# A fixed order for TensorE in the RWKV-7 recurrence of a decoder trunk: small products behind each chain step, then four dense k-tiles

## The chip, the cores and the metric

The kernel runs on one core of a Trainium2 chip. The metric is the device time of one execution in microseconds (us). A run of the same program is repeated, and the median is taken. The kernel before the change takes 2544.87 us (median of three runs, 2544.0 to 2546.05).

## What is computed

A two-layer decoder trunk over 256 tokens with 2048 channels, in float32: an RWKV-7 time mixing layer, then a causal differential attention layer, each followed by a gated MLP with a short convolution, with layer norms between. The change lies wholly in the time mixing, whose core is this:

```python
def wkv7_scan(r, decay, k, v, a_vec, b_vec):
    def step(S, inp):
        r_t, w_t, k_t, v_t, a_t, b_t = inp
        sa = jnp.einsum('bhij,bhj->bhi', S, a_t)
        S = S * w_t[:, :, None, :] + sa[..., None] * b_t[:, :, None, :] + v_t[..., None] * k_t[:, :, None, :]
        y = jnp.einsum('bhij,bhj->bhi', S, r_t)
        return S, y
...
def rwkv7_mix(x, ...):
    r = xr @ w_rkv[0]; k = xk @ w_rkv[1]; v = xv @ w_rkv[2]
    w = -softplus(-(w0 + tanh(xw @ w1) @ w2)) - 0.5
    a = sigmoid(a0 + (xa @ a1) @ a2); g = sigmoid(xg @ g1) @ g2
    ...
    y = wkv7_scan(r_h, decay, k_h, v_h, -kk, kk * a_h)
    ...
    return (y * g) @ w_o
```

The r, k and v weights are 2048 by 2048; the scan runs over 32 heads of 64 channels, with `kk` normalised per head before it and a group norm per head and a bonus term behind it.

## The kernel before

**Dense products.** A 2048-wide product is cut into k-tiles of 128 rows. Each weight tile comes from memory as float32 (`raw`, by SyncE's queue), ScalarE (ACT) rounds it to TensorE's shorter float (fp32r) (`hi`, line 213), VectorE (DVE) forms the rest (`lo`, line 216), and TensorE (PE) multiplies. One `hi` and one `lo` tile hold two k-tiles; each of the three pools has six buffers in this part, so `lo` can run at most twelve k-tiles ahead. A k-tile costs PE either three matmuls of 256 columns (lines 224 to 226: twice with `hi`, once with `lo`; the r and k products of the recurrence) or one of 512 and one of 256 (lines 228 and 229; the output product w_o). The third of the first kind, line 226, is the one that needs `lo`.

**The recurrence.** The 2048 channels are handled in eight groups of 256 (four heads). A group passes four stages, written as Python generators that `yield` between steps:

- `products(g)` (line 1075): the r and k products of the group, 64 dense k-tiles, 20 steps.
- `front(g)` (line 1085): the elementwise work of the group, mostly on DVE with 512-wide tiles: norm of k (product of line 1107), decay factors, the scaled operands `KB` (lines 1139, 1140) and `AR` (1141, 1143); then 32 products of line 1152 that fill the chunk matrices `M` (DVE, line 1155). It also runs two of the three small low-rank products of a group (`lora`, line 822: lines 224 to 226 with the operand `mid`).
- `lanes(g)` (line 1188): the inverse of the triangular chunk matrices: four transposes (line 1211, twice), tiny DVE steps (1215, 1217), a trip through memory (1220, 1224), and six rounds of 16 or 32 tiny products (lines 1238, 1247, 1259, 1266, 1277, 1286), each round waiting for a copy or a transpose of the one before on ACT or DVE (the first for 1231, the second for the masking of line 1239).
- `chain(g)` (line 1308) and `outputs(g)` (line 1391): the four chunks of 64 tokens one after the other. Per chunk the products of lines 1353/1357 (with the state `S`) or 1342, a copy to `R`, line 1365, a copy to `UV`, line 1376 and a new `S` on DVE (1380, 1383), with 1386 adding to the result. Thirteen steps, each waiting for a copy of the one before. Then the group norm: line 1407 on PE, and on DVE and ACT 1409, 322 to 326, 1413, 1414. For the last three groups line 1414 is followed by the split of the result into `S1`, the operand of w_o (lines 194 and 195).

`pipeline` (line 1009) runs in round i the chain of group i, the lanes of i+1, the front of i+2 and the products of i+3 together. `_together` takes the next step of whichever generator has the smallest share done, by the step counts in `PACE`. In the last three rounds `early(n)` (line 1024) takes the place of the products: parts of the first fourteen columns of w_o whose inputs are already there.

**What sets the order.** The framework reorders at compile time: from the written program, its priorities and its own cost table it fixes one order of instructions per engine, and each engine executes its list in that order. All waits are semaphores put in by the framework. The low-rank products share one buffer each for the raw and the split weights (`lb=1`): the split of one (lines 828 on ACT, 830 on DVE) writes the buffer which the matmuls of the one before read. Small products of `front` and `lanes` write to a ring of two PSUM banks (`pst`).

The lines that call the scheduler's helper and set the pace, the rest being printed below:

```python
PACE = dict(chain=37.24, front=19.56, lanes=19.55, products=40.92, pool=0, pool0=0, chain0=0, front0=0,
...
    def pst(self):
        return self.pss.tile([P, 2 * T], F32, name="pss")
```

Of the kernel before, what the change touches and what calls it, by code (L numbers as in the profile page):

```python
# [14 lines left out]
P = 128  # L15
# [13 lines left out]
NC = T // C  # L29
GT = 2  # L30
NG = KT // GT
WCH = 4
HCH = 2
PACE = dict(chain=37.24, front=19.56, lanes=19.55, products=40.92, pool=0, pool0=0, chain0=0, front0=0,
            lanes0=0, early0=0, products0=0, wc='AVVA', ek='AA', ez='VA', ec='AVAA', ey='V', el='V', w0=(3, 4,
            4), lb=1, early=46.23, vw=(6, 6, 6), vp=2, ep='V', eg='A', lg=2, lr=2, la=4, ah=10, ao=12, ah0=0.05)
EARLY = {j: 0 if j < 5 else 1 if j < 11 else 2 for j in range(14)}
AGAIN = (2,)
ORDER = [0, 1, 14, 2, 3, 4, 5, 6, 7, 15, 8, 9, 10, 11, 12, 13]
# [89 lines left out]
class Trunk:  # L129
    def __init__(self, ctx, tc, a):  # L130
# [5 lines left out]
        self.wp = []  # L136
        self.weight_pools(ctx, "0", PACE["w0"])
        self.tmp = mk("tmp", 3)
# [478 lines left out]
    def attention(self, lead=None, ahead=None):  # L617
        nc, tc = self.nc, self.tc
        with ExitStack() as ctx:
# [18 lines left out]
            def query_steps(h, n=0):  # L638
                evac = queries(h)
                yield from self.dense_steps(self.qk_blocks(h)[n:], KT, self.S0, lambda j, ps: evac(j + n, ps))  # L640

            def values(h):
                def evac(ps):
                    vt = ap.tile([P, 2, 2, P], F32, name="vt")
                    nc.scalar.copy(out=vt, in_=ps.rearrange("p (a b c) -> p a b c", a=2, b=2))
                    qkv[h].append(vt)

                yield from self.token_steps(self.a["da_v"][h], self.S0, evac)
# [89 lines left out]
    def rwkv(self, ahead=None):  # L738
        nc, tc = self.nc, self.tc
        with ExitStack() as ctx:  # L740
# [192 lines left out]
def _all(steps):  # L933
    for _ in steps:
        pass


def _then(*steps):
    for s in steps:
        yield from s  # L940


def _together(*todo):

    at = [[o[0] if o else 0.0, i, s, 1.0 / n] for i, (s, n, *o) in enumerate(todo)]
    while at:
        m = min(at)
        try:
            next(m[2])
            m[0] += m[3]  # L950
        except StopIteration:
            at.remove(m)
# [10 lines left out]
class Groups:  # L963
# [44 lines left out]

    def pipeline(self):
        for i in range(-3, NG):  # L1010
            todo = []
            if i >= 0:
                todo.append((_then(self.chain(i), self.outputs(i)), PACE["chain"], PACE["chain0"]))
            if 0 <= i + 1 < NG:
                todo.append((self.lanes(i + 1), PACE["lanes"], PACE["lanes0"]))
            if 0 <= i + 2 < NG:
                todo.append((self.front(i + 2), PACE["front"], PACE["front0"]))
            if 1 <= i + 3 < NG:
                todo.append((self.products(i + 3), PACE["products"], PACE["products0"]))
            if i + 3 >= NG:  # L1020
                todo.append((self.early(i - (NG - 3)), PACE["early"], PACE["early0"]))
            _together(*todo)

    def early(self, n):

# [162 lines left out]
    def lanes(self, g):  # L1188

        t, nc, g1 = self.t, self.nc, self.g1  # L1190
        s = self.st[g]
        M, d1, d2, KB, pc = s["M"], s["d1"], self.d2, s["KB"], s["pc"]
        KBT = s["KBT"] = self.g2.tile([P, GT * NC, P], F32, name="KBT")
# [11 lines left out]
                                in1=pc.rearrange("p j c o -> p (j c) o").broadcast_to([P, GT * NC, 2 * C]),  # L1205
                                op=ALU.mult)
        yield
        for u in range(0, GT * NC, 4):
            ps = self.pst()
            for w in range(4):  # L1210
                nc.tensor.transpose(out=ps[:, w * P:(w + 1) * P], in_=KB[:, u + w, :, :], identity=t.c("ident"))
            self.copy(PACE["ek"][u // 4], KBT[:, u:u + 4, :].rearrange("p u c -> p (u c)"), ps)
            yield
        for i in range(1, 8):
            nc.vector.tensor_tensor(out=tt[:, :i, :i], in0=Tl[:, :i, :i],
                                    in1=Ml[:, 0:i, i].unsqueeze(1).broadcast_to([P, i, i]), op=ALU.mult)
# [4 lines left out]
        for par in range(2):  # L1221
            for be in range(2):
                r0 = (64 if par == 0 else 0) + 32 * be
                nc.sync.dma_start(out=W1[r0:r0 + 32],
                                  in_=self.dram(d2, par * 8, ((C, 32), (4 * DBL, 8), (1, 32)), at=be * 2 * DBL))
# [7 lines left out]
        ps = self.pst()  # L1233
# [9 lines left out]
        ps = self.pst()  # L1243
# [10 lines left out]
        ps = self.pst()  # L1254
# [7 lines left out]
        ps = self.pst()  # L1262
# [10 lines left out]
        ps = self.pst()  # L1273
# [8 lines left out]
        ps = self.pst()  # L1282
# [207 lines left out]
```

## Time and profile before

| what | value |
|---|---|
| median of three runs | 2544.87 us |
| the profiled execution's own time | 2540.27 us |
| its span from first to last instruction | 2537.5 us |
| mean granted TensorE clock | 0.99 |
| busy: PE / DVE / ACT | 2461.7 / 2030.6 / 1648.8 us |
| first product of line 1407 (output of group 0) | 277.51 us after the start of the span |
| last product of line 1407 (group 7) | 593.45 us |

Times in views are microseconds from the start of the span. PE means matmuls, PEld its weight loads. A matmul's own duration overlaps the next one's: in a stream the distance between starts counts, not the duration. An engine's "idle before" names what ended the idle time. In the table of stretches each engine has its busy time and the number of its instructions, then the granted clock and the load of the DMA engines. The eight products of line 1407 mark the rounds of the pipeline.

### The profile page before, as it was taken

What the parts mean: (1) busy time and instruction counts of PE and PEld (TensorE: products, weight loads), DVE (VectorE), ACT (ScalarE), POOL (GpSimd) and SP (SyncE); (2) the same over time, 40 slices, a digit from 0 to 9 for tenths busy, and PEclk for the clock granted to TensorE, in tenths of its full rate; (3) what the DMA queues carried; (4) which work ended last, traced back from release to release, by engine and by line L of the source; (5) the groups of instructions that cost most, each with busy time, mean ns of one, the idle gap of its engine ahead of it and who ended that gap; (6) DMA issues with size and microseconds to landing.
All of it is one profiled execution on the core that took longest, in us unless ns stands there. A gap on an engine that the chain in (4) does not pass through costs nothing.

```text
span 2537.5 us, 56569 instructions
## 1 busy us (share of the span) xinstructions
PE 2461.7 (97%) x18622; PEld 2170.2 (86%) x18622; DVE 2030.6 (80%) x5192; ACT 1648.8 (65%) x4334; POOL 172.0 (7%) x236
## 2 busy tenths in 40 slices
PE   7999999999899999999999999999999999999996
PEld 6988888777888888888889899988988888888886
DVE  8988888878997777776776977779887777776776
ACT  5766566545676666665666666666766666666664
POOL 1000000000300000000111200003300000000111
PEclk9999999999999999999999999999999999999998
DMA  6644343344465556666766455556465555566664
GB/s 189 187 141 120 110 108 102 106 127 125 133 198 189 190 190 190 190 190 196 215 188 188 149 167 174 171 176 184 147 198 188 188 188 188 188 187 186 188 190 128
DMA packets 276743, 428.70 MB, mean 169 GB/s; under 512 B 60632, under 2 KB 83168, under 8 KB 276448
## 3 DMA queue, kind: packets, MB, share of 16 engines
q1 hardware_dynamic: 276448, 425.10, 55.6%
q8 instruction: 145, 2.38, 0.4%
q14 instruction: 150, 1.23, 0.2%
HBM read 420.25 MB, written 6.31 MB: 168 GB/s over the span
## 4 chain that ended last, share of the span: by engine, by line
PE 81%; DVE 3%; ACT 1%; DMA 1%; issue 1%; SPq 0%; POOL 0%; ACTq 0%; DVEq 0%; POOLq 0%
PE psd L228 43%; PE psd L229 22%; PE psd L224 2%; PE psd L225 2%; PE psd L226 2%; PE psd L296 1%; PE psd L295 1%; PE psd L294 1%; PE psd L900 1%; PE psd L899 1%; PE psd L901 1%; DVE lo L216 1%; DMA raw<-in_rw_o 1%; PE lnst L348 1%; PE pss L1152 0%
## 5 line engine op out<-in xcount | busy, mean ns | idle before, releaser
L213 ACT CAST hi<-raw 128x256 fp32r<-128x256 f32 (+1 forms) x3128 | 1231.4, 404 | 682.1 <-PE psd L228 466.2
L216 DVE TENSOR_TENSOR lo<-raw,hi 128x256 fp32r<-128x256 f32 (+1 forms) x3124 | 1308.3, 430 | 418.9 <-ACT hi L213 375.9
L228 PE MATMUL psd<-S,hi 128*128 128x512 f32 x3004 | 1056.7, 396 | 0.8 <-DVE S L195 0.8
L229 PE MATMUL psd<-S,lo 128*128 128x256 f32 x3004 | 842.1, 280 | 3.9 <-DVE lo L216 3.8
L228 PEld LDWEIGHTS psd<-S,hi 128*128 128x128 f32 x3004 | 566.2, 189 | 132.8 <-ACT hi L213 1.3
L229 PEld LDWEIGHTS psd<-S,lo 128*128 128x128 f32 x3004 | 566.0, 188 | 5.6 <-DVE lo L216 5.3
L228 PE MATMUL psd<-hs,hi 128*128 128x512 f32 x1290 | 451.2, 394 | 0.0
L229 PE MATMUL psd<-hs,lo 128*128 128x256 f32 x1290 | 361.5, 280 | 0.0
L228 PEld LDWEIGHTS psd<-hs,hi 128*128 128x128 f32 x1290 | 241.8, 187 | 56.3 <-ACT hi L213 0.9
L229 PEld LDWEIGHTS psd<-hs,lo 128*128 128x128 f32 x1290 | 243.1, 188 | 0.4 <-DVE lo L216 0.3
L226 PE MATMUL psd<-S,lo 128*128 128x256 f32 x480 | 139.1, 290 | 2.9 <-DVE lo L216 2.8
L224 PE MATMUL psd<-S,hi 128*128 128x256 f32 x480 | 138.5, 289 | 1.6 <-ACT hi L213 1.4
L225 PE MATMUL psd<-S,hi 128*128 128x256 f32 x480 | 137.6, 287 | 0.0
L228 PE MATMUL psd<-S1r,hi 128*128 128x512 f32 x276 | 107.2, 419 | 2.0 <-ACT hi L213 1.0
L226 PEld LDWEIGHTS psd<-S,lo 128*128 128x128 f32 x480 | 90.7, 189 | 8.6 <-DVE lo L216 5.0
L224 PEld LDWEIGHTS psd<-S,hi 128*128 128x128 f32 x480 | 90.7, 189 | 6.4 <-ACT hi L213 2.3
L225 PEld LDWEIGHTS psd<-S,hi 128*128 128x128 f32 x480 | 90.6, 189 | 1.7 <-issue 1.4
L366 POOL COPY ln_acc<-X 128x256 f32<-128x256 f32 x4 | 2.0, 512 | 1239.3 <-DVE X L400 1239.3
L224 PE MATMUL psd<-S1r,hi 128*128 128x256 f32 x284 | 85.6, 301 | 0.0
L900 PE MATMUL psd<-S,lo 128*128 128x258 f32 x256 | 77.7, 303 | 8.1 <-DVE lo L216 8.1
L228 PE MATMUL psd<-S1a,hi 128*128 128x512 f32 x240 | 84.9, 398 | 0.0
L229 PE MATMUL psd<-S1r,lo 128*128 128x256 f32 x276 | 80.8, 293 | 1.5 <-DVE lo L216 1.5
(303 smaller groups left out, 3577.3 us busy)
## 6 DMA issues: line engine op xcount, KB each, us to landing
raw<-in_ff_up SPq DMA_DIRECT2D x676, 256.0 KB, 3.4
raw<-in_ff_down SPq DMA_DIRECT2D x320, 256.0 KB, 3.0
raw<-in_rkv SPq DMA_DIRECT2D x192, 256.0 KB, 3.6
raw<-in_da_qk SPq DMA_DIRECT2D x122, 256.0 KB, 3.4
raw<-in_da_v SPq DMA_DIRECT2D x64, 256.0 KB, 3.0
raw<-in_da_o SPq DMA_DIRECT2D x64, 256.0 KB, 3.7
raw<-in_rw_o SPq DMA_DIRECT2D x50, 256.0 KB, 3.3
raw<-in_ff_down SPq DMA_DIRECT2D x32, 192.0 KB, 2.6
```

What stands on the lines that cost most here:

```text
L213: nc.scalar.copy(out=hi[:, :s * P], in_=r)
L216: eng.tensor_tensor(out=lo[:, :s * P], in0=r, in1=hi[:, :s * P].bitcast(F32), op=ALU.subtract)
L224: nc.tensor.matmul(ps[:, :T], lhsT=hi, rhs=xs[:, :T], start=first, stop=False)
L225: nc.tensor.matmul(ps[:, :T], lhsT=hi, rhs=xs[:, T:], start=False, stop=False)
L226: nc.tensor.matmul(ps[:, :T], lhsT=lo, rhs=xs[:, :T], start=False, stop=last)
L228: nc.tensor.matmul(ps, lhsT=hi, rhs=xs, start=first, stop=False)
L229: nc.tensor.matmul(ps[:, T:], lhsT=lo, rhs=xs[:, :T], start=False, stop=last)
L294: nc.tensor.matmul(o, lhsT=xh, rhs=hi, start=k == 0 and b == 0, stop=False)
L295: nc.tensor.matmul(o, lhsT=xh, rhs=lo, start=False, stop=False)
L296: nc.tensor.matmul(o, lhsT=xl, rhs=hi, start=False, stop=k == KT - 1 and b == T // P - 1)
L348: self.nc.tensor.matmul(st, lhsT=self.c("onesd"), rhs=t, start=not self.ln_open and n == 0, stop=stop and n == 1)
L900: nc.tensor.matmul(ps[:, 2:4 + T], lhsT=lo[:, w], rhs=x[:, 2:4 + T], start=False, stop=False)
```

## The change

In rounds 0 to 7 TensorE keeps the order in which the source creates its instructions (`manual_schedule`); the other engines are still ordered by the framework. The source's order is rewritten: `abreast` takes one step of the chain (or of the outputs behind it), then steps of the lanes at a rate of 12/17 and of the front at 16/17 per chain step; `_together` sets this against the products with 18 and 20 steps, so that four dense k-tiles follow each chain step. `early` gets one step count for each of its three rounds. In `lanes` the two banks of transposes are issued together, and the copies behind them. Code below the change moves down: line numbers of `lanes`, `front` and `chain` grow by 16 to 18.

```diff
-PACE = dict(chain=37.24, front=19.56, lanes=19.55, products=40.92, pool=0, pool0=0, chain0=0, front0=0,
+PACE = dict(chain=18, front=19.56, lanes=19.55, products=20, pool=0, pool0=0, chain0=0, front0=0,
...
     def pipeline(self):
         for i in range(-3, NG):
-            todo = []
-            if i >= 0:
-                todo.append((_then(self.chain(i), self.outputs(i)), PACE["chain"], PACE["chain0"]))
+            todo, side = [], []
             if 0 <= i + 1 < NG:
-                todo.append((self.lanes(i + 1), PACE["lanes"], PACE["lanes0"]))
+                side.append((self.lanes(i + 1), PACE["lanes"], PACE["lanes0"]))
             if 0 <= i + 2 < NG:
-                todo.append((self.front(i + 2), PACE["front"], PACE["front0"]))
+                side.append((self.front(i + 2), PACE["front"], PACE["front0"]))
             if 1 <= i + 3 < NG:
                 todo.append((self.products(i + 3), PACE["products"], PACE["products0"]))
             if i + 3 >= NG:
-                todo.append((self.early(i - (NG - 3)), PACE["early"], PACE["early0"]))
-            _together(*todo)
+                n = i - (NG - 3)
+                todo.append((self.early(n), PACE["early"][n], PACE["early0"]))
+            if i < 0:
+                _together(*side, *todo)
+            else:
+                with self.t.tc.manual_schedule(engines={mybir.EngineType.PE}):
+                    _together((self.abreast(_then(self.chain(i), self.outputs(i)), [s for s, *_ in side]), PACE["chain"],
+                               PACE["chain0"]), *todo)
+
+    def abreast(self, main, side):
+
+        rates = dict(zip(side, (12 / 17, 16 / 17)) if len(side) > 1 else ((s, 12 / 17) for s in side))
+        due = dict.fromkeys(side, 0.0)
+        for _ in main:
+            for s in side:
+                due[s] += rates[s]
+                while due[s] >= 1:
+                    next(s, None)
+                    due[s] -= 1
+            yield
+        _all(_then(*side))
...
-        for u in range(0, GT * NC, 4):
-            ps = self.pst()
-            for w in range(4):
-                nc.tensor.transpose(out=ps[:, w * P:(w + 1) * P], in_=KB[:, u + w, :, :], identity=t.c("ident"))
-            self.copy(PACE["ek"][u // 4], KBT[:, u:u + 4, :].rearrange("p u c -> p (u c)"), ps)
-            yield
+        banks = [self.pst(), self.pst()]
+        for u in range(GT * NC):
+            nc.tensor.transpose(out=banks[u // 4][:, u % 4 * P:(u % 4 + 1) * P], in_=KB[:, u, :, :],
+                                identity=t.c("ident"))
+        for u, ps in enumerate(banks):
+            self.copy(PACE["ek"][u], KBT[:, 4 * u:4 * u + 4, :].rearrange("p u c -> p (u c)"), ps)
+        yield
```

**Place 1: DVE in the middle of the front of one group (steady rounds).** Before, DVE's list between the second copy to `R` and the fill of the scaled operands reads so; `lo_` with a number is one `lo` tile, `AR`, `wa`, `k`, `KB` are tiles of the front, `UV` and `R` belong to the chain.

```order
L1059 COPY R_2553<-b1_5502 128x64
L1127 SCALAR_TENSOR_TENSOR kk_5449<-k_4620,par_74,kk_5449 128x256
L1129 TENSOR_SCALAR t1_5448<-wa_5342,par_74 128x256
L1141 SCALAR_TENSOR_TENSOR AR_5444<-kk_5449,Lx_5532 128x8x64
L1132 TENSOR_TENSOR wa_5342<-kk_5449,wa_5342 128x512
L1133 SCALAR_TENSOR_TENSOR k_4620<-t1_5448,k_4620 128x512
L1059 COPY UV_2552<-us_5426 64x128
L216 TENSOR_TENSOR lo_5688<-raw_5685,hi_5687 128x256
L216 TENSOR_TENSOR lo_5698<-raw_5685,hi_5697 128x256
L216 TENSOR_TENSOR lo_5720<-raw_5717,hi_5719 128x256
```

The same place in the changed kernel, from the last `lo` tile ahead of these operations to the first behind them:

```order
L216 TENSOR_TENSOR lo_5642<-raw_5629,hi_5641 128x256
L1149 TENSOR_TENSOR wa_5167<-kk_5511,wa_5167 128x512
L1150 SCALAR_TENSOR_TENSOR k_4605<-t1_5510,k_4605 128x512
L1157 TENSOR_TENSOR KB_5667<-wa_5167 128x2x2x64
L1076 COPY UV_2552<-us_5434 64x128
L1156 TENSOR_TENSOR KB_5667<-k_4605,wa_5167 128x2x2x64 x2
L1157 TENSOR_TENSOR KB_5667<-wa_5167 128x2x2x64
L1158 SCALAR_TENSOR_TENSOR AR_5506<-kk_5511,Lx_5562 128x8x64
L1160 TENSOR_TENSOR AR_5506<-r_4999,eL_5563 128x8x64
L216 TENSOR_TENSOR lo_5677<-raw_5674,hi_5676 128x256
```

The three `lo` tiles which stood ahead of the four `KB` operations and the second `AR` operation now stand behind them. What PE has in its list between the last matmul with `lo_5642` and the first with `lo_5677` is this:

```order
L226 MATMUL psd_5444<-S0_76,lo_5642 128x256
L1383 MATMUL us_5434<-R_2553,M_3833 64x64 x4
L1360 MATMUL b0_5489<-UV_2552,M_3833 64x64 x2
L1360 MATMUL b1_5490<-UV_2552,M_3833 64x64 x2
L224 MATMUL psd_5444<-S0_76,hi_5676 128x256
L225 MATMUL psd_5444<-S0_76,hi_5676 128x256
L226 MATMUL psd_5444<-S0_76,lo_5677 128x256
```

Here one step of the chain (lines 1365 and 1342 of the kernel before) and two dense matmuls are all that stands between the two.

**Place 2: PE at the second and third low-rank product of a round.** Before, the second product (`mid0`, weights `l2_6179`) and the third (`mid1`, `l2_6236`) have other small products between them:

```order
L226 MATMUL psd_6183<-mid0_81,l2_6179 128x256
L1318 MATMUL us_6261<-ext_2531,X_75 128x128 x2
L1323 MATMUL us_6261<-ext_2531,X_75 64x128
L1277 MATMUL pss_6193<-T1_6190,M_4612 32x32 x16
L224 MATMUL psd_6240<-mid1_82,l2_6236 128x256
```

In the changed kernel they follow each other:

```order
L224 MATMUL psd_6086<-mid2_83,l2_6082 128x256
L225 MATMUL psd_6086<-mid2_83,l2_6082 128x256
L226 MATMUL psd_6086<-mid2_83,l2_6082 128x256
L224 MATMUL psd_6098<-mid1_82,l2_6094 128x256
L225 MATMUL psd_6098<-mid1_82,l2_6094 128x256
```

`l2_6082` and `l2_6094` are the same buffer, so the second's weights can be split only when the first's six matmuls are through.

**Place 3: PE behind the last product of line 1407.** Before, dense k-tiles of w_o follow whose inputs are there (`psd_9660`, and after it `psd_9688` and others, 44 k-tiles in all):

```order
L1407 MATMUL us_9747<-o_y2_9674,ext_2531 128x512
L228 MATMUL psd_9660<-S1r_80,hi_9663 128x512
L229 MATMUL psd_9660<-S1r_80,lo_9664 128x256
L228 MATMUL psd_9660<-S1r_80,hi_9663 128x512
L229 MATMUL psd_9660<-S1r_80,lo_9664 128x256
```

Now the k-tiles of the last group's own result follow at once (`psd_9975` and `psd_9989`, the first two columns of w_o):

```order
L1425 MATMUL us_9922<-o_y2_9835,ext_2531 128x512
L224 MATMUL psd_9975<-S1r_80,hi_9978 128x256
L224 MATMUL psd_9989<-S1r_80,hi_9992 128x256
L225 MATMUL psd_9975<-S1r_80,hi_9978 128x256
L226 MATMUL psd_9975<-S1r_80,lo_9979 128x256
```

The 44 k-tiles have moved ahead of line 1425, between the steps of the last chain.

More of the change, by code (lines that the diff above doesn't have):

```diff
@@ L33 @@
 HCH = 2
-PACE = dict(chain=37.24, front=19.56, lanes=19.55, products=40.92, pool=0, pool0=0, chain0=0, front0=0,
+PACE = dict(chain=18, front=19.56, lanes=19.55, products=20, pool=0, pool0=0, chain0=0, front0=0,
             lanes0=0, early0=0, products0=0, wc='AVVA', ek='AA', ez='VA', ec='AVAA', ey='V', el='V', w0=(3, 4,
-            4), lb=1, early=46.23, vw=(6, 6, 6), vp=2, ep='V', eg='A', lg=2, lr=2, la=4, ah=10, ao=12, ah0=0.05)
+            4), lb=1, early=(16, 25, 34), vw=(6, 6, 6), vp=2, ep='V', eg='A', lg=2, lr=2, la=4, ah=10, ao=12, ah0=0.05)
 EARLY = {j: 0 if j < 5 else 1 if j < 11 else 2 for j in range(14)}
```

## The prediction

> **What bounds the kernel now.** I read the page first:
>
> ```profile
> PE 2461.7 (97%) x18622; PEld 2170.2 (86%) x18622; DVE 2030.6 (80%) x5192; ACT 1648.8 (65%) x4334; POOL 172.0 (7%) x236
> ```
>
> PE is busy for 97%, so time goes where PE's list gets shorter, or where it waits. Outside the recurrence the order is unchanged, so I cut that part at the first products of line 1407 (before's numbers), one round per row; the last row runs from the eighth to PE's first product behind the recurrence.
>
> ```profile
> 277.51:325.67 48.16, 46.88 (x758) 40.20 (x757) 41.32 (x109) 30.67 (x74) 0.69 (x3) 1.00 0.41 108
> 422.19:470.66 48.47, 46.60 (x759) 40.06 (x757) 42.48 (x111) 32.95 (x78) 0.69 (x3) 1.00 0.40 107
> 470.66:514.59 43.93, 40.64 (x470) 30.69 (x469) 37.95 (x105) 26.15 (x64) 0.46 (x3) 1.00 0.37 106
> 514.59:563.99 49.40, 48.69 (x848) 37.17 (x847) 35.01 (x99) 23.56 (x60) 0.00 (x0) 0.90 0.46 123
> 593.45:617.55 24.10, 20.30 (x111) 16.19 (x109) 19.75 (x52) 11.87 (x31) 0.10 (x1) 1.00 0.54 158
> ```
>
> The first two rows are the first and last of four steady rounds: 193.15 us from 277.51 to 470.66, 48.3 each. PE is idle there for 1.3 and 1.9 us, and DVE is busy for 41 to 42 of the 48: a second engine with little room. PE's waits in the four rounds:
>
> ```profile
> PE pss L1286 <- ACT T L1279: 3.1, 4, 0.9
> PE pss L1107 <- DVE bon L1175: 1.1, 4, 0.3
> PE pss L1247 <- DVE M L1155: 0.6, 2, 0.3
> PE b L1353 <- DVE S L1383: 0.4, 1, 0.4
> ```
>
> These sum to 5.2, or 1.3 per round: all that waiting costs in the order of before.
>
> The rest of PE's time is its work, and in its timeline one sees what cutting the dense stream costs:
>
> ```profile
> 397.94 0.45 PE L1376 MATMUL us<-UV,KBT 128*64 128x64 f32 x8
> 398.22 0.40 PE L1386 MATMUL yps<-M,UV 128*64 128x64 f32 x8
> 398.55 0.38 PE L224 MATMUL psd<-S,hi 128*128 128x256 f32 x1
> 398.78 0.28 PE L225 MATMUL psd<-S,hi 128*128 128x256 f32 x1
> 398.90 0.28 PE L226 MATMUL psd<-S,lo 128*128 128x256 f32 x1
> ...
> 399.97 0.28 PE L226 MATMUL psd<-S,lo 128*128 128x256 f32 x1
> 400.18 0.34 PE L1353 MATMUL b<-S,AR 64*64 64x64 f32 x8
> ```
>
> Dense matmuls start 0.12 apart (398.78 to 398.90), but the first is followed after 0.23 and the last after 0.21. So a piece costs 0.09 to 0.11 at each end, 0.2 in all, beside its matmuls. This piece, four k-tiles, takes 1.63 (398.55 to 400.18).
>
> **The change part by part.** *Removed.* The 64 k-tiles of a round stood in some 20 pieces and stand in 15: five pieces by 0.2 is 1.0 less. The new order puts four k-tiles ahead of most products that waited, so the 1.3 of waits may go too. At most 2.4 per round (0 at the worst). I take 2.4.
>
> *Added: DVE's block in the front (Place 1).* DVE executes its list in order. Here are its operations as they ran before:
>
> ```profile
> 395.17 0.68 DVE L1141 SCALAR_TENSOR_TENSOR AR<-kk,Lx 128x512 f32<-128x512 f32 x1
> 395.77 0.68 DVE L1132 TENSOR_TENSOR wa<-kk,wa 128x512 f32<-128x512 f32 x1
> 396.38 0.68 DVE L1133 SCALAR_TENSOR_TENSOR k<-t,k 128x512 f32<-128x512 f32 x1
> 397.09 0.29 DVE L1059 COPY UV<-us 64x128 f32<-64x128 f32 x1
> 397.42 1.10 DVE L216 TENSOR_TENSOR lo<-raw,hi 128x256 fp32r<-128x256 f32 x3
> 398.54 0.47 DVE L1380 SCALAR_TENSOR_TENSOR S<-S,pc,us 128x64 f32<-128x64 f32 x2
> 398.94 0.41 DVE L216 TENSOR_TENSOR lo<-raw,hi 128x256 fp32r<-128x256 f32 x1
> 399.27 0.42 DVE L1139 TENSOR_TENSOR KB<-k,wa 128x256 f32<-128x256 f32 x1
> 399.61 0.42 DVE L1140 TENSOR_TENSOR KB<-wa 128x256 f32<-128x256 f32 x1
> ```
>
> From start to start a 512-wide operation takes 0.60 (395.17 to 395.77), a 256-wide one 0.34 (399.27 to 399.61), a small copy about 0.25 (0.33 here, to 397.42). Before, three `lo` tiles ran in the middle (397.42) and two around the `KB`. Now there are none from `lo_5642` to `lo_5677`: `wa`, `k`, four `KB`, the copy to `UV`, two `AR` take 2x0.60 + 4x0.34 + 0.25 + 2x0.60 = 4.0, and `lo_5677` itself 0.41, less the 0.08 by which an operation outlasts the distance to the next one (0.42 against 0.34): 4.3 between the end of the one tile and the end of the other. PE has in its list between them: two k-tiles with `lo_5642` (about 0.6), lines 1365 and 1342 (0.4, as for 1376 and 1386 together above: 0.6 at most), the two matmuls with `hi` (0.35), 1.35 in all. It stalls for 4.3 - 1.35 = 3.0.
>
> Could DVE be ahead, so that nobody waits? A copy to `R` stands ahead of `lo_5642` in its list, and that needs PE's product of line 1353, only four k-tiles (1.63) earlier. So the lead is at most what fits behind this copy, and I take 3.0 whole; the lower bound is 0, if that product runs much earlier than it stands. Behind the waiting matmul of line 226 the chain's 1376 is queued too, so nothing passes by.
>
> *Added: two low-rank products back to back (Place 2).* The second's split needs the one buffer free, that is, the first's last matmul through. Then ACT and DVE have to do this:
>
> ```profile
> L828 ACT CAST l<-l2r 128x256 fp32r<-128x256 f32 x12 | 4.9, 408 | 0.2
> L830 DVE TENSOR_TENSOR l<-l2r,l 128x256 fp32r<-128x256 f32 x12 | 5.0, 418 | 0.0
> L1239 DVE TENSOR_TENSOR Z<-pss,ext 128x128 f32<-128x128 f32 x4 | 1.2, 292 | 0.2
> ```
>
> 0.41 + 0.42, with three hand-overs between engines of about 0.1 each (estimate, as 0.09 to 0.11 above): 1.2 is the least that PE waits. Ahead of line 828 in ACT's list stand five copies and activations, each like the row of 828 (0.41) or a little longer; PE's products release some of them only now. Three more make 1.2 + 3x0.45 = 2.6 the upper end. I take 2.1: two of the five.
>
> *Added: three short ones.* Line 1353 follows 1376 with only 1386 between (0.33, 398.22 to 398.55) while `S` needs 1380 and 1383 first (0.47 + 0.28 by their kind of rows): 0.5 (0.25 to 0.75). Line 1152 stands straight behind the 32 products of 1238, whose second PSUM bank DVE still has to empty by line 1239 (0.29 and two hand-overs): 0.5 (0.3 to 0.8). `lo_5642` comes late itself, behind the copy to `R`: 0.3 (0 to 0.6).
>
> Together 3.0 + 2.1 + 0.5 + 0.5 + 0.3 = 6.4 against 2.4 removed: **+4.0 per round**, in the five rounds (0 to 4) in which PE's order repeats: **+20**. Bounds: least 0 + 1.2 + 0.25 + 0.3 + 0 = 1.75, so -0.65 per round; most 3.0 + 2.6 + 0.75 + 0.8 + 0.6 = 7.75 with nothing removed, +7.75.
>
> *The clock.* A new stall can cost a second time:
>
> ```profile
> 235.09:238.50 3.41, 2.36 (x41) 1.81 (x41) 2.14 (x5) 3.33 (x7) 0.00 (x0) 1.00 0.35 106
> 238.50:241.91 3.41, 3.41 (x10) 2.38 (x11) 2.61 (x10) 2.44 (x5) 0.00 (x0) 0.50 0.02 5
> 525.22:535.46 10.24, 10.24 (x97) 6.67 (x96) 5.79 (x15) 4.63 (x12) 0.00 (x0) 0.50 0.37 100
> 648.10:651.51 3.41, 1.36 (x5) 0.91 (x6) 3.41 (x8) 2.22 (x6) 1.69 (x4) 1.00 0.81 225
> 651.51:654.92 3.41, 3.41 (x17) 3.14 (x16) 2.85 (x8) 1.82 (x5) 0.00 (x0) 0.50 0.84 219
> 649.97 0.70 PE L348 MATMUL lnst<-ln_acc,cst 128*128 128x256 f32 x2 [2.47 <-POOL ln_acc L373]
> ```
>
> Column three is PE's busy time, the 1.00 or 0.50 the granted clock. After a stretch with 1.36 of 3.41 busy, whose longest idle time was 2.47, the clock was halved for 3.41 us, which costs up to 3.41/2 = 1.7 us of PE time. At 235.09 a stretch with 2.36 busy was enough. A stall of 3.0 is as long. But whether it falls into one stretch hangs on how the stretches lie: I estimate two in three, 1.7 x 2/3 x 5 = +5.7, taken as **+5** because PE isn't dense all through such a stretch. The Trainium skill, TensorE: Matmul & The Clock Gate, in Part 1 (The HAM clock gate), has the clock halved only after a whole idle window of about 3.4 us; by that rule a stall of 3.0 would bring nothing and these +5 would be 0. The trace speaks against it: 2.47 us of idle time were enough at 649.97.
>
> *The last three rounds.* Before loses 3.3 of the 43.93 from 470.66 (PE busy 40.64) and, by the stretch at half clock from 525.22, 5.1 of the 10.24. After has its own losses there: the same DVE block in round 5, and short distances from 1259 to 1266 and 1277 to 1286 in round 6. I take 0, with 8 either way.
>
> *The tail (Place 3).* Before, 48 k-tiles follow the last line 1407, and hide the last group's norm. Now four do, and they need that norm's result.
>
> ```profile
> 593.45 1.09 PE L1407 MATMUL us<-o_y,ext 128*128 128x512 f32 x2
> 566.00 0.63 ACT L322 ACTIVATE Lx<-o_y 128x512 f32<-128x512 f32 x1
> 567.48 0.69 DVE L324 TENSOR_TENSOR Lx<-o_rs 128x512 f32<-128x512 f32 x1
> ```
>
> These are one row of line 1407 and, from the group before, samples of the steps behind it. Up to the first operand of w_o there are six such steps on DVE (1409, 324, 325, 326, 1413, 1414; 0.69 each) and three on ACT (322, 323, 194; 0.63 each): 1.09 + 6x0.69 + 3x0.63 = 7.1 in which PE has no work, all new; line 195 comes beside the first matmuls. Against it stands what before loses in its last 24.10 us (PE busy 20.30, so 3.8 idle, and slow k-tiles for want of weights, 1.3 as estimate): 7.1 - 5.1 = +2. The clock after 7 us idle is halved, by the rows above, up to 2 us more: **+4** (0 to +8).
>
> Sum: 20 + 5 + 0 + 4 = +29. The profiled execution took 2540.27, so 2569.3; it ran 4.60 below the median of 2544.87, to which the same +29 gives **2574**.
>
> **The rivals.**
>
> *No half clock* after the new stalls: 29 - 5 = +24, 2569. Its mechanism: a stall of 3.0 lies across the border of two stretches of 3.41, so that each keeps about 1.9 of 3.41 busy. For it speaks this stretch, less busy than the one at 235.09, behind which the clock stayed whole:
>
> ```profile
> 211.19:214.60 3.41, 2.14 (x14) 1.77 (x14) 3.06 (x8) 1.82 (x6) 0.00 (x0) 1.00 0.70 169
> 214.60:218.02 3.42, 3.02 (x27) 2.67 (x28) 3.42 (x10) 1.95 (x5) 0.00 (x0) 1.00 0.18 62
> ```
>
> Against it speak the two cases above. The Trainium skill's rule (same page and part) gives the same 2569 by another reason, the length of the idle time.
>
> *Heavier:* both stalls, in front and low-rank products, halve the clock each time: 2 x 1.7 x 5 = 17 instead of 5, +41, 2586; with the upper bound of the low-rank wait and tail (+2.5, +4) 2592.
>
> *DVE's lead covers the block:* the 3.0 go, and so does the clock: 5 x 1.0 + 4 = +9, 2554; with a tail at 0 it is 2550 and beside no change. It decides whether line 1353 runs ahead by over 3 us of its place in the dense stream.
>
> *Faster:* the regular order does what its form says. The waits that come sum to the lower bound: 5 x -0.65 = -3.3; the 3.3 and 5.1 lost from 470.66 and 525.22 come back, since four k-tiles follow every step and no idle stretch halves the clock; tail +4. -3.3 - 8.4 + 4 = -7.7, 2537. For it: every wait shown above is behind a chain step with too little between. Point of decision: new waits under 2.4 per round. Against it: DVE's list at Place 1.
>
> **How the numbers follow.** Forecast 2574: 0.43. No half clock: 0.18. Heavier: 0.10. DVE's lead covers: 0.13, of which 0.08 beside no change. Faster: 0.16. A measurement of this kernel can tell about 0.2%, 5 us, from no change: 2540 to 2550. Faster 0.16, same 0.08, slower 0.43 + 0.18 + 0.10 + 0.05 = 0.76. The range leaves out most of the faster case and what lies above the heavier one: 2540 to 2598.
>
> **What would show it right or wrong.** Right: the distance between line 1425's products (1407 before) is 52 to 54 in steady rounds; PE's waits name line 226 on DVE's `lo` with about 3 per round, and lines 224 or 226 of a low-rank product on `l` with about 2; granted clock below 1.00 in some of these stretches; PE idle for about 7 us behind the last line 1425. Wrong: a distance of 48 or less; no wait on `lo` over 1 us; or these waits as forecast, with the losses of rounds 5 to 7 gone.

## The result, and the profile after

| | before | changed |
|---|---|---|
| median of the runs compared | 2545.45 us (4 runs) | 2612.05 us (4 runs) |
| ratio, 95% interval | | 1.026 (1.0242 to 1.0278) |
| the profiled execution's own time | 2540.27 us | 2608.99 us |
| its span / mean granted clock | 2537.5 us / 0.99 | 2607.2 us / 0.971 |

The change makes the kernel 66.6 us slower. The forecast had +29, and a range up to 2598. The rounds again, from one first product of line 1425 (1407 before) to the next; the columns are length, then busy time and count of PE, PEld, DVE, ACT and POOL, the granted clock, and the DMA's share and rate:

```profile
298.58:357.21 58.63, 51.60 (x758) 45.38 (x757) 41.81 (x109) 30.94 (x74) 0.42 (x3) 0.85 0.34 92
357.21:411.68 54.47, 47.47 (x759) 41.70 (x758) 41.45 (x109) 30.81 (x74) 0.39 (x3) 0.94 0.34 92
411.68:468.74 57.06, 50.05 (x758) 44.04 (x757) 41.57 (x109) 30.84 (x74) 0.39 (x3) 0.88 0.33 90
468.74:528.72 59.98, 52.97 (x758) 46.83 (x757) 43.02 (x109) 32.60 (x77) 0.39 (x3) 0.84 0.34 89
```

Four rounds take 230.14 us in place of 193.15: 57.5 each, 9.25 more. PE is idle for 7.0 in each (58.63 - 51.60, and so on), where it was 1.6. And the clock, 1.00 in all four before, is below 0.95 now. PE's waits in these four rounds:

```profile
PE psd L226 <- DVE lo L216: 11.7, 4, 2.9
PE psd L224 <- ACT wa L1322: 9.0, 4, 2.2
PE psd L224 <- ACT o_rs L1076: 3.9, 4, 1.0
PE b L1371 <- DVE S L1401: 2.8, 4, 0.7
```

Of the four waits shown of before three are gone and that for `S` has grown (0.4 to 2.8); with three new ones it is 6.85 us per round, where it was 1.3. The first is the block of DVE of Place 1, in DVE's timeline and PE's:

```profile
373.22 0.68 DVE L1149 TENSOR_TENSOR wa<-kk,wa 128x512 f32<-128x512 f32 x1
...
376.78 0.68 DVE L1160 TENSOR_TENSOR AR<-r,eL 128x512 f32<-128x512 f32 x1
377.38 1.42 DVE L216 TENSOR_TENSOR lo<-raw,hi 128x256 fp32r<-128x256 f32 x4
```

```profile
377.85 0.38 PE L226 MATMUL psd<-S,lo 128*128 128x256 f32 x1 [2.92 <-DVE lo L216]
```

From `wa` at 373.22 to the first `lo` behind `AR` at 377.38 lie 4.16 us without a `lo` tile, and PE waits for 2.92 of them. The second and third wait are at the low-rank products of Place 2. PE's timeline, then ACT's:

```profile
400.78 0.58 PE L224 MATMUL psd<-mid,l 128*128 128x256 f32 x1 [2.25 <-ACT wa L1322]
403.41 0.58 PE L224 MATMUL psd<-mid,l 128*128 128x256 f32 x1 [0.98 <-ACT o_rs L1076]
```

```profile
396.53 1.28 ACT L1322 ACT_TABLE_LOAD   x1
397.83 0.47 ACT L1322 ACTIVATE wa<-psd,par 128x256 f32<-128x256 f32 x1
398.20 0.70 ACT L213 CAST hi<-raw 128x256 fp32r<-128x256 f32 x2
398.80 0.26 ACT L1076 COPY W<-pss 128x128 f32<-128x128 f32 x1
398.96 0.61 ACT L1419 ACTIVATE o_y<-yps 128x512 f32<-128x512 f32 x1
399.45 0.80 ACT L1076 COPY M<-W 32x256 f32<-32x256 f32 x2
400.26 0.47 ACT L1322 ACTIVATE wa<-psd,par 128x256 f32<-128x256 f32 x1
402.47 0.40 ACT L828 CAST l<-l2r 128x256 fp32r<-128x256 f32 x1 [1.74 <-PE psd L226]
402.78 0.58 ACT L1076 COPY o_rs<-psd 128x512 f32<-128x512 f32 x1
```

PE does not wait here for the split of line 828, which the forecast named. It waits for the second sigmoid (400.26), which reads the first product's PSUM bank, and then for the copy to `o_rs` (402.78), which reads the second's. The dense products and the low-rank ones share a ring of two banks, and the dense product under way holds one of them. ACT goes without a pause from the table load at 396.53 (1.28 us) through the first sigmoid and six other operations to the second.

Behind these stalls the clock is halved. Three stretches of 3.41 us with what follows:

```profile
314.70:318.11 3.41, 1.56 (x22) 1.16 (x22) 3.38 (x8) 0.77 (x3) 0.00 (x0) 1.00 0.43 101
318.11:324.94 6.83, 5.71 (x43) 5.15 (x44) 4.34 (x13) 1.72 (x4) 0.00 (x0) 0.50 0.30 96
...
512.67:516.08 3.41, 1.11 (x22) 0.81 (x10) 2.89 (x7) 2.32 (x8) 0.00 (x0) 1.00 0.25 73
516.09:529.74 13.65, 12.73 (x109) 11.64 (x109) 6.42 (x14) 8.33 (x18) 0.00 (x0) 0.50 0.16 45
...
376.14:379.55 3.41, 1.70 (x20) 1.56 (x22) 3.22 (x9) 0.70 (x2) 0.00 (x0) 1.00 0.10 31
379.55:382.96 3.41, 3.41 (x57) 3.09 (x52) 3.10 (x8) 1.76 (x5) 0.00 (x0) 1.00 0.65 171
```

Of the eight large stalls of the four rounds, seven have such a stretch behind them, of 6.83 to 13.65 us; only the one at 376 has none. By the clocks of the four rounds, 2 x (1 - 0.85) x 58.63 and so on, PE runs at half clock for 57 us of the 230; it is busy for 49 of these and loses at most half of that, 24.5, or 6.1 per round. So a round is 7.0 idle + at most 6.1 clock + at least 44.4 of work at full clock, where it was 1.6 + 0 + 46.7. The same cut is used for the experiments; the first of them gives the clock's share without that halving, 5.1 per round.

The last stretches, from the eighth product to PE's first behind the recurrence among them:

```profile
627.60:676.40 48.80, 41.88 (x347) 32.49 (x346) 33.25 (x89) 21.06 (x56) 0.00 (x0) 0.93 0.32 100
676.40:688.22 11.82, 4.04 (x16) 2.99 (x15) 8.67 (x19) 3.40 (x7) 0.10 (x1) 0.65 0.39 114
```

From the fifth product of line 1425 at 528.72 to 688.22 it takes 159.5 us; before it was 617.55 - 470.66 = 146.9. Of PE's 26 us idle there 7.8 are the one wait behind 676.40 (for `S1`, line 194), and 4.7 one in the last round (for group 6's `S1`, line 195). In sum: 21.1 up to the first product of line 1425 (298.58 against 277.51), 37.0 in rounds 1 to 4, 12.6 after them, together 70.7; 1.0 comes back behind the recurrence and 1.0 lies outside the span, which leaves 68.7.

### The profile page after: what moved, and what is told of

It reads as the page before. It is cut to its first block, busy times and chain, and to the rows that moved or that the text cites. A ratio compares the mean times of both kernels' runs of the same rounds, so it can differ in the third digit from the quotient of the medians.

```text
span 2607.2 us, 56561 instructions
## 1 busy us (share of the span) xinstructions
PE 2479.5 (95%) x18622; PEld 2194.0 (84%) x18622; DVE 2033.8 (78%) x5192; ACT 1649.6 (63%) x4334; POOL 172.0 (7%) x236
## 3 DMA queue, kind: packets, MB, share of 16 engines
q1 hardware_dynamic: 276448, 425.10, 54.5%
## 4 chain that ended last, share of the span: by engine, by line
PE 75%; DVE 3%; ACT 1%; issue 1%; DMA 1%; POOL 0%; ACTq 0%; DVEq 0%; POOLq 0%
PE psd L228 42%; PE psd L229 21%; PE psd L294 1%; PE psd L296 1%; PE psd L295 1%; PE psd L224 1%; PE psd L900 1%; PE psd L901 1%; PE psd L899 1%; PE psd L226 1%; PE psd L225 1%; DVE lo L216 1%; DMA raw<-in_rw_o 1%; PE lnst L348 1%; PE pss L659 0%
## 5 line engine op out<-in xcount | busy, mean ns | idle before, releaser
L224 PE MATMUL psd<-S,hi 128*128 128x256 f32 x480 | 144.8, 302 | 2.1 <-ACT hi L213 2.1
L225 PE MATMUL psd<-S,hi 128*128 128x256 f32 x480 | 138.2, 288 | 0.0
L224 PE MATMUL psd<-S1r,hi 128*128 128x256 f32 x284 | 90.6, 320 | 7.8 <-ACT S1r L194 7.8
L226 PE MATMUL psd<-S1r,lo 128*128 128x256 f32 x284 | 85.5, 301 | 1.7 <-DVE lo L216 1.5
L229 PE MATMUL psd<-S1r,lo 128*128 128x256 f32 x276 | 80.7, 292 | 6.0 <-DVE lo L216 6.0
L225 PE MATMUL psd<-S1r,hi 128*128 128x256 f32 x284 | 84.8, 299 | 0.0
```

Of the source, the lines that this page charges most:

```text
L224: nc.tensor.matmul(ps[:, :T], lhsT=hi, rhs=xs[:, :T], start=first, stop=False)
L225: nc.tensor.matmul(ps[:, :T], lhsT=hi, rhs=xs[:, T:], start=False, stop=False)
L226: nc.tensor.matmul(ps[:, :T], lhsT=lo, rhs=xs[:, :T], start=False, stop=last)
L229: nc.tensor.matmul(ps[:, T:], lhsT=lo, rhs=xs[:, :T], start=False, stop=last)
```

## The experiments

Each was compared with runs of the kernel before on the same chip (medians of 2538 to 2541), so ratios to it are compared; "against the kernel before" is that ratio.

**fill_stalls.** Matmuls that nobody reads, where PE would stand still: 24 behind the chain's second step, 8 and 18 ahead of the second and third low-rank product.

```diff
+    def fill(self, n):
+        x = self.t.S0[:, 0, :]
+        for _ in range(n if self.rb else 0):
+            self.nc.tensor.matmul(self.rb[0][:, T:], lhsT=x[:, :P], rhs=x[:, :T], start=True, stop=True)
...
+            if c == 1 and g < 6:
+                self.fill(24)
```

> The changed kernel with matmuls that nobody reads at the places where PE stalls in rounds 0 to 5: 24 of 0.12 us (2.9 us) behind the second chain step, 8 and 18 (1.0 and 2.1 us) ahead of the second and third low-rank product. PE's other work and the orders of DVE and ACT are as in the changed kernel. Theory A (each stall also halves the clock, and that is the second half of the loss): the waits on lo and on the low-rank weights shrink to under 0.7 each, the half-clock windows of rounds 0 to 5 (about 73 us of them in the trace of the changed kernel) mostly vanish, and the kernel gets 22 to 33 us faster, 2579 to 2590, although PE has 6 us more to do per round. Rival B (only the idle time costs, the half clock falls on time that is lost anyway): no change, 2608 to 2616.

Measured: ratio 1.0204 (1.0189 to 1.0219). One of the steady rounds, and the largest waits in the four:

```profile
349.89:403.25 53.36, 51.38 (x809) 45.77 (x808) 41.39 (x109) 30.85 (x74) 1.91 (x3) 1.00 0.38 97
```

```profile
PE psd L224 <- ACT wa L1329: 4.2, 4, 1.1
PE b L1378 <- DVE S L1410: 3.1, 4, 1.0
```

The clock is 1.00 through all four rounds, and a round takes 53.5 in place of 57.5, with 50 matmuls (6.0 us) more in it. This is theory A's mechanism, with a smaller gain than expected (about 14 in place of 22 to 33), outside the ranges of both theories. One reason is that fill and remaining waits together are longer than the old stalls: 6.0 + 2.0 idle against 7.0. That half clock costs time of its own, beside the idle time that starts it, is shown, and its size too: PE is busy for 51.4 per round here, 45.4 without the fill (50 x 0.12), and was for 50.5 in the changed kernel. The 5.1 between are the clock, about 20 us in the four rounds, and PE's own work shrank from 46.7 to 45.4.

**lo_first.**

```diff
-            eng.tensor_tensor(out=lo[:, :s * P], in0=r, in1=hi[:, :s * P].bitcast(F32), op=ALU.subtract)
+            with self.tc.high_priority(100) if self.urgent else ExitStack():
+                eng.tensor_tensor(out=lo[:, :s * P], in0=r, in1=hi[:, :s * P].bitcast(F32), op=ALU.subtract)
```

> The changed kernel, with the lo split of the weights given a higher priority for DVE in rounds 0 to 7; PE's order is the same row for row. DVE is then eight k-tiles further when the block of wa, k, KB and AR begins. Theory A: the wait of 2.9 us on lo in rounds 0 to 5 goes (-17), and the half-clock windows behind it go too (-15 to -18): 2577 to 2583. Rival B: -17 alone, 2594 to 2597. Rival C (the block only moves: another wait on DVE comes late instead, the state S or the copies of the chain): less than -10, 2602 or more, with new waits on DVE of 2 us and more per round.

Measured: 1.0232 (1.0217 to 1.0248). PE's waits in the four rounds:

```profile
PE pss L1173 <- DVE AR L1164: 14.0, 4, 3.5
PE psd L226 <- ACT wa L1326: 9.0, 4, 2.2
```

The wait on `lo` is gone, and one of 3.5 on `AR` is there (line 1152 of before). Rival C holds: it is not the order within DVE's list that falls short but DVE's time. PE's order leaves DVE too little between the group's first product and line 1152, whichever work comes first.

**lora_two_buffers.** `lb=1` becomes `lb=2`.

> The changed kernel with two buffers for the low-rank weights in place of one; PE's order in the rounds is the same. Theory A: the waits of 3.2 us per round ahead of the second and third low-rank product go in rounds 0 to 5 (-17), and the half-clock windows behind them (6.8 to 13.7 us long) go too (-18 to -22): 2573 to 2580. Rival B: -17 alone, about 2595. Rival C (the split is late because ACT's and DVE's queues are, not because the buffer is taken): half of the wait stays, and with it the half clock: 2600 to 2608.

Measured: 1.0265 (1.024 to 1.029), nothing gained:

```profile
PE psd L226 <- DVE lo L216: 11.7, 4, 2.9
PE psd L224 <- ACT wa L1322: 9.0, 4, 2.2
```

The wait on the sigmoid stays to the tenth, which none of the three theories foresaw; that on the copy to `o_rs` falls from 3.9 to 2.7. So the buffer of the weights was not what PE waited for first, and the releaser that the row names, `wa`, is to be taken at its word.

**lo_first_two_buffers.** Both edits.

> Both: lo with priority and two buffers. PE's order in the rounds as in the changed kernel. Theory A: both stalls and their half clock go, -60 to -70 together: 2543 to 2555; what is left against the kernel before is the last two rounds and the tail (+13 in the trace), less the five dense pieces and the waits that the new order saves per round (2.4 x 5 = -12). Rival B: -34, about 2578. Rival D (the order itself costs, four k-tiles behind each step being too little for the chain's copies): waits on S and UV of over 1 us per round remain and the time stays over 2560.

Measured: 1.019 (1.0174 to 1.0205). The waits of both runs above remain (3.5 on `AR`, 2.2 on `wa`), and so the 60 us do not come. What is gained is clock: each round has one half-clock stretch of 6.8 in all instead of 14.3 on average.

**lora_own_banks** and **lora_own_banks_two_buffers.** The second and third product go to the chain's banks, the latter run with `lb=2` too:

```diff
-        ps = self.psum()
+        ps = bank() if bank else self.psum()
...
-            yield from t.lora(self.lp, self.mids, g, i, banks.append)
+            yield from t.lora(self.lp, self.mids, g, i, banks.append, (lambda: self.bank("b1")) if i else None)
...
-        yield from t.lora(self.lp, self.mids, g, 2, lambda ps: self.copy(PACE["eg"], _fl(rs), ps))
+        yield from t.lora(self.lp, self.mids, g, 2, lambda ps: self.copy(PACE["eg"], _fl(rs), ps),
+                          lambda: self.bank("b0"))
```

> The changed kernel, with the second and third low-rank product of a round written to the chain's two idle banks b0 and b1 in place of the ring of two that the dense products use. PE's order in the rounds is the same; the weights keep their one buffer. Theory E (PE waits there for a PSUM bank, which the second sigmoid sets free; its place in ACT's list is behind six other operations): the waits on the sigmoid and on the copy to o_rs (3.2 us per round) go, in their place comes the wait for the split of the third product's weights, 1.2 to 2 us; PE's half-clock stretches behind them partly go: 15 to 25 us less than the changed kernel, that is, +42 to +52 against the kernel before. Rival F (the split of the weights is what is late, as forecast, and the sigmoid only ends at the same time): nothing gained, +62 to +70.

> The run lora_own_banks with two buffers for the low-rank weights as well. Theory E: now no wait over 0.5 us is left at these products, 25 to 35 us less than the changed kernel, +32 to +42 against the kernel before; the wait on lo (2.9) and its half clock stay. Rival F: as with two buffers alone, +62 to +70.

Measured: 1.0181 (1.0166 to 1.0196) and 1.013 (1.0113 to 1.0146). PE's waits in the four rounds, with one buffer and then with two:

```profile
PE psd L226 <- DVE lo L216: 11.7, 4, 2.9
PE b L224 <- ACT l L828: 2.6, 4, 1.1
PE b L1371 <- DVE S L1401: 2.6, 4, 0.6
PE b L226 <- DVE l L830: 2.2, 3, 0.7
```

```profile
PE psd L226 <- DVE lo L216: 11.7, 4, 2.9
PE b L1371 <- DVE S L1401: 3.6, 4, 1.0
```

Theory E holds. With the bank free, the split of the weights comes to light: (2.6 + 2.2)/4 = 1.2 per round, the least that the forecast had worked out. With two buffers that goes as well. A round then takes 51.05: 4.2 idle, at most 1.9 clock, 44.9 work; the stall on `lo` alone halves the clock less often and for less time:

```profile
338.84:389.81 50.97, 46.67 (x758) 41.02 (x757) 41.26 (x109) 30.39 (x74) 0.40 (x3) 0.97 0.36 102
```

**front_spread_own_banks.** Two more `yield`s in `front`, rates `(12 / 17, 18 / 17)`.

> Own banks and two buffers, and the block of DVE in the front cut by two more yields (before wa and before AR), the front's rate raised from 16/17 to 18/17: lo tiles stand between the parts, and the products of line 1152 stand one chain step later. Theory A with E: both stalls and nearly all half clock of rounds 0 to 5 go; a round takes 45 to 47 us, less than the 48.3 before, since PE's own work in it is 44.5 us (the changed kernel's round less its idle time and half clock); the last two rounds and the tail still lose 13: -5 to +10 against the kernel before. Rival C (DVE has too little room wherever the block stands): a wait on DVE of over 2 us per round is left, with half clock, +25 or more.

Measured: 1.0181 (1.0166 to 1.0196), worse than without the spreading:

```profile
PE pss L1258 <- DVE T L1251: 17.4, 4, 4.6
PE psd L226 <- DVE lo L216: 6.6, 12, 1.2
```

Rival C again: the wait on `lo` shrinks to 1.65 per round, and the inverse's first products (line 1238 before) wait 4.35 for DVE's tiny steps, which the front has pushed back.

**source_order_not_fixed** and **old_order_fixed.** The first leaves `manual_schedule` away from the changed kernel; the second puts it alone into the kernel before.

> The changed source without manual_schedule: the framework may move PE's instructions again. Theory G (the loss comes from fixing PE's order, with DVE's and ACT's lists made from a cost table that sees no stall there): the framework moves waiting products back, and the time is within 10 us of the kernel before. Rival H (the source's order is the loss, fixed or not): +40 or more.

> The kernel before, with PE's order in rounds 0 to 7 fixed to that of its own source (manual_schedule alone; step counts, chain, front and lanes as before). Theory G (fixing PE lets stalls through which the framework's own order avoids): waits on DVE and ACT of 2 us and more per round, half clock behind them, +20 to +70. Rival H (only the new order's places are bad): within 10 us of the kernel before.

Measured: 1.011 (1.0095 to 1.0125) and 1.0117 (1.0099 to 1.0136). The largest waits in the four rounds of each:

```profile
PE pss L1169 <- DVE AR L1160: 6.3, 4, 1.6
PE us L1394 <- DVE UV L1076: 2.9, 4, 0.7
```

```profile
PE pss L1251 <- DVE M L1159: 6.8, 4, 1.7
PE pss L1290 <- DVE T L1284: 5.1, 4, 1.3
```

The first run fits neither of its theories: the new source order costs 28 us even when the framework may move it. The second comes out as theory G expected: fixing costs 30 with the old order, with waits on DVE and ACT and half clock. Both together cost 66, so neither the order nor the fixing alone is the loss. PE waits mostly for DVE, a round takes 51.8 and 54.5, and half clock is a part (at most 2.5 and 4.0 per round).

**tail_k_tiles_later** and **last_round_reordered.** `early=(16, 25, 34)` becomes `(16, 25, 24)`; and

```diff
-        for j, m in EARLY.items():
+        for j, m in sorted(EARLY.items(), key=lambda e: n == 2 and e[1] != n):
```

> The changed kernel with the third step count of early lowered from 34 to 24, so that fewer k-tiles of w_o follow each step of the last chain and 28 instead of 4 stand behind the last product of line 1425. If the last group's norm is what PE waits 7.8 us for there: that wait goes, 6 to 9 us less than the changed kernel (+57 to +61 against the kernel before). Rival (the k-tiles are missed between the steps of the last chain instead): waits there grow by as much, +64 to +68.

> The changed kernel; in the last round early takes the three columns of w_o first that begin with inputs long there, and only then the eleven that need group 6's result at once. If the wait of 4.7 us for that result (line 195) and the half clock behind it (2.9) are a loss of their own: 5 to 8 us less than the changed kernel, +58 to +62 against the kernel before. Rival (it moves the wait to the end of the round, where more k-tiles of group 7 or the norm are awaited): +64 or more.

Measured: 1.0233 (1.0216 to 1.0251) and 1.0233 (1.0214 to 1.0251). From the fifth product of line 1425 on they take 151.2 and 150.2 in place of 159.5, and each keeps the other's wait:

```profile
PE psd L228 <- DVE S1r L195: 4.7, 1, 4.7
```

```profile
PE psd L224 <- ACT S1r L194: 7.0, 1, 7.0
```

So the two waits are losses of their own, 8.3 and 9.3 us with their half clock. Together that is more than the 12.6 lost. A part of the difference is work that has moved: PE runs 140 matmuls more ahead of the first product of line 1425 than it did ahead of 1407 (2589 against 2449), and about as many fewer from the fifth on. They take about 3 us, an estimate from 0.72 for 64 small ones and 0.8 for each of two low-rank products. The rest was not looked into. The ratios alone, whose intervals touch that of the changed kernel, would not show it as surely as these traces.

**block_eased, block_eased_spread, and both reordered.** Own banks, two buffers, the later tail; `ep='A'` (the copies of the r and k products go from DVE to ACT), priority for the tiny steps, and one or two yields. What each of these brings is not told apart.

```diff
-            4), lb=1, early=(16, 25, 34), vw=(6, 6, 6), vp=2, ep='V', eg='A', lg=2, lr=2, la=4, ah=10, ao=12, ah0=0.05)
+            4), lb=2, early=(16, 25, 24), vw=(6, 6, 6), vp=2, ep='A', eg='A', lg=2, lr=2, la=4, ah=10, ao=12, ah0=0.05)
...
+            with t.tc.high_priority(200):
+                nc.vector.tensor_tensor(out=tt[:, :i, :i], in0=Tl[:, :i, :i],
+                                        in1=Ml[:, 0:i, i].unsqueeze(1).broadcast_to([P, i, i]), op=ALU.mult)
```

> Own banks and two buffers, k-tiles of the tail later, and DVE's first half of the round eased: the copies of the r and k products go to ACT (1.4 us per round), the inverse's tiny steps have priority, and one yield stands before AR (front's rate 17/17); PE's order keeps line 1152 where it is. Theory A with E: the wait on lo falls below 1.2 us and no half clock is left in rounds 0 to 4, a round takes 46 to 47.5; -8 to +5 against the kernel before. Rival C: DVE's first half is still too long by over 2 us, a round takes 49 or more; +10 to +20.

> As block_eased, with two yields (before wa and before AR) at 18/17, so that line 1152 stands one chain step later. Theory A with E: the 4.6 us for the inverse's first products, which came in front_spread_own_banks, go with the priority; waits per round under 1.5 us, no half clock, a round of 45.5 to 47; -12 to 0 against the kernel before. Rival C: another wait on DVE of 2 us or more takes the place; +5 to +20.

> The run block_eased with the same order of early in the last round. If both losses are independent: 5 to 8 us less than block_eased, -6 to 0 against the kernel before, the first version of the new order that is faster. Rival: no less than block_eased (+3 to +8), because the last round then waits elsewhere.

> The run block_eased_spread with the order of early of last_round_reordered. If the gain of that order adds: 3 to 8 us less than block_eased_spread, -8 to -3 against the kernel before, faster than both. Rival (the last round then waits for S or for group 7 instead): within 3 us of the kernel before.

Measured, in this order: 1.0021 (1.0011 to 1.0032), 0.9999 (0.9987 to 1.0011), 1.0011 (1.0 to 1.0023), 0.9987 (0.9976 to 0.9998). The last, 3 us below the kernel before, is the only one whose interval lies below 1, and it all but touches. The order of `early` was expected to bring 5 to 8 and 3 to 8 us; it brought about 2.5 and 3, with intervals that overlap. In the last of these runs a round takes 48.7: 2.9 idle, at most 0.8 clock, 45.0 work, against 1.6, 0 and 46.7; in three of the four rounds the clock is 1.00, and PE is busy there for 45.1. What the waits still hold:

```profile
PE psd L226 <- DVE lo L216: 6.8, 8, 1.1
PE b L1374 <- DVE S L1404: 4.4, 4, 1.8
```

Theory A with E is right on the 4.6 us (gone) and the clock (nearly), and the rounds (49.0 and 49.2 in the first two) come out 1.5 to 2.2 us above the upper ends that it expected: waits for `lo` and `S` of (6.8 + 4.4)/4 = 2.8 per round are left. The new order pays in PE's work (1.6 per round) and gives it back in waits for DVE; what it wins against the kernel before, it wins in the last rounds (139.9 in place of 146.9), and about 3 of these 7 are the products that moved ahead of round 0's end.

## Why the prediction was wrong

- **The direction and the path were right**: PE waits for DVE's block, for the low-rank products and for `S`. The waits that come were 6.4 per round in the forecast and are 6.85 in the trace. Without the clock a round is 4.1 longer (9.25 - 5.1) where +4.0 was forecast; that the sum fits so well is in part luck, since its terms miss both ways.
- **DVE's block**: 3.0 forecast, 2.9 measured, with its mechanism. lo_first adds what the forecast had not: the `lo` tiles' place is only one of the two forms of the loss.
- **The low-rank products**: 2.1 forecast, 3.2 measured, and the named cause failed. "The second's split needs the one buffer free" is true, but two buffers gained nothing, and the bank came first. The rows of ACT's list ahead of the waiting product were counted; which of them frees something that PE writes was not asked.
- **The three short ones**: 1.3 forecast; 0.7 for `S`, and nothing for 1152 and the late `lo`.
- **Removed**: 2.4 forecast; the 1.6 of idle time went and 1.3 of work (46.7 to 45.4, by fill_stalls), 2.9. Five pieces by 0.2, the 1.0 forecast, come near that 1.3.
- **The clock, the step that failed**: "I estimate two in three, 1.7 x 2/3 x 5 = +5.7, taken as +5". In rounds 1 to 4 alone it was about 20 (fill_stalls; 24.5 at most), and in round 0 two more single stretches and one of 6.83 came. Three things were missed: both stalls of a round halve the clock, not one (seven of eight); a stretch lasts 6.83 us or more in these rounds, not 3.41, as the prediction's own row of 10.24 at 525.22 could have warned; and PE is busy in most of it (49 of 57), so that nearly all of it costs. fill_stalls shows that these us are real. Here the Trainium skill, TensorE: Matmul & The Clock Gate, Part 1, would have misled further: by its whole idle window of about 3.4 us there would be no half clock, and the trace has it behind stretches in which PE was busy for 1.11 and 1.56 of 3.41, with no idle time over 2.93 in those rounds.
- **Round 0** was taken as one of five alike (+5); the time up to its last product is 21.1 longer. Of these 3.9 are there at the first chain step (line 1365 first at 246.41 before, 1383 at 250.31 now): the run-up changed too, which the forecast left at nothing, and PE waits there 6.6 us for `AR` in place of 2.6. Of the rest, 17, the waits of this round are 8.0, its half clock is up to 6.3, and about 3 are the 140 matmuls that stood behind this mark before.
- **The last three rounds and the tail**: 0 + 4 forecast, 12.6 measured. The wait in the tail was right (7.1 against 7.8). What was missed is the wait for group 6's result in the last round (4.7 and its half clock), where `early` asks for it first: 9.3 by last_round_reordered. About 3 us of moved work hide a part of it in the 12.6.
- **The rivals**: "Heavier" came nearest. It had both stalls halve the clock, at 1.7 each, so 2586 to 2592; with the 2.9 that a stretch cost here (20 over seven) in place of the 1.7 its clock term is 2 x 2.9 x 5 = 29 in place of 17, and its sum 2598 to 2604. The rest up to 2612 is the run-up and the last rounds.
- **In sum**, the trace lost 68.7 where 29 was forecast. Of the 40 missing, some 16 are the clock in rounds 1 to 4, 16 the time up to round 0's end and 9 the last rounds; 2 of these 41 come back.

## What to carry to other kernels

A stall on TensorE is to be priced twice: its own length, and the work that then runs at half clock, here 5.1 us per round on 7.0 of stalls. The waits before the change, none over 0.9 us in these rounds, left the clock whole. Where PE's order is fixed and the other engines' lists are not, sum up each other engine's work between two fixed products before asking in which order it stands: moving a wait is easy, and shortening it takes work off that engine. And of a waiting product, ask first which operation frees the PSUM bank that it writes.

## What the runs showed of the hardware

The busy share of a stretch of 3.41 us did not alone decide the clock. After 1.70 busy at 376.14 it stayed whole, while after this stretch, with more, it was halved:

```profile
427.34:430.75 3.41, 2.01 (x26) 1.40 (x24) 3.38 (x10) 1.07 (x3) 0.00 (x0) 1.00 0.42 110
430.75:437.58 6.83, 5.25 (x42) 4.91 (x42) 4.69 (x12) 1.72 (x4) 0.00 (x0) 0.50 0.28 82
```

Both are the same stall of 2.9 us in two rounds, cut differently by the stretches. Why the one counts and the other does not stays open.

The length of a half-clock stretch has a pattern. In all seven of the four rounds PE still has idle time in the first 3.41 us (busy for 1.68 to 2.81) and is busy throughout the next 3.41. Five of them end there, after 6.83. The other two, at 345.42 and 516.09, go on for another 3.41 and 6.83 although PE is busy all through; why stays open.
